# Two feed-forward layers of a float32 encoder trunk, rewritten with Strassen's seven products

## The chip, the cores and the metric

The kernel runs on one core of a Trainium2 chip. The metric is the device time of one execution in microseconds (us). PE is TensorE, DVE is VectorE, ACT is ScalarE, POOL is GpSimd and SP is SyncE, whose queue issues most of the loads.

## The reference

The trunk has two layers on 528 tokens (16 meta tokens, then 512 frames) of width 1024. Layer 0 is multi-scale retention, layer 1 is attention over a shared compressed key and value. Each ends with a dense feed-forward of hidden width 2816:

```python
def swiglu(hn, w1, w3, w2):
    return (jax.nn.silu(hn @ w1) * (hn @ w3)) @ w2

h = h + swiglu(rmsnorm(h, norm_ffn_g[layer]), ffn_w1[layer], ffn_w3[layer], ffn_w2[layer])
```

After layer 1 only the 512 frames are kept, and a last RMSNorm gives the output. All is float32.

## The kernel before

Activations are transposed: features on the 128 partitions (8 tiles for the width, 22 for the hidden width) and tokens along the free axis. A float32 product is three float32r passes over operands that are split into a head and a rest (`split`, L210 to L213: an ACT copy gives the head at L212, a DVE subtraction gives the rest at L208). Weights come as raw tiles of 128x1024 through SP's queue and are split the same way. The ring of weight tiles (`weight_tiles`) has three buffers each for raw, head and rest.

A product (`gemm`) runs over tiles of 128 output columns m. For each m it takes all tiles k of the contraction, and for each k three matmuls (`mm`): for all 528 tokens each is issued in two halves of 264 columns (L246), for 512 frames at once (L248). One matmul has its own weight load in every case.

The feed-forward (`ffn`) has two parts of 11 hidden tiles. Each part computes 22 column tiles of w1 and w3 in turn (`up`), with `evac` after each pair: two DVE products from PSUM with the norm's scale, a Silu on ACT, a DVE product and a split. Then it multiplies with half of w2 (8 column tiles, 11 hidden tiles each) and `add` adds to `h[m]`. In layer 0 the second part's additions are each followed by `prep_mla`, which makes the next stage's operands. In layer 1 the second part is `finish`: the last product, the final norm and the output for half of the frames, then for the other half. In front of the feed-forwards, `prep_ffn` follows the last addition to each `h[m]` in the projections of retention and attention.

The engines' instruction order is made by a scheduler from the program's dependencies and priorities. It isn't the order of the program's text. Semaphores and the reuse of tile buffers come from the same tool.

Before the feed-forwards stand the retention (four heads, some 480 us) and, between the two, the attention (eight heads, some 280 us). In them the change touches memory pools, the shape of some temporary tiles and the order of a few steps.

Of the kernel before, what the change touches and what calls it, by code (L numbers as in the profile page):

```python
# [42 lines left out]
SLOTS = 57  # L43
# [4 lines left out]
# Steps of other work at five places of each head's attention.  # L48
# [9 lines left out]
class Filler:  # L58
    """Steps of independent work, to be put between the steps of a chain."""
# [22 lines left out]
class Head:  # L82
    """One head's attention over tiles of 128 queries, in stages."""
# [37 lines left out]
    def weights(self, i):  # L121
        """The probabilities with keys on partitions, split."""
        k, nc, p = self.k, self.nc, self.p[i]
        qs = slice(i * P, (i + 1) * P)
        if i == 0:
            self.ph = k.tp.tile([P, 4, SEQ], F32R, tag="pth", name=k.name("pth"), bufs=1)
            self.pl = k.tp.tile([P, 4, SEQ], F32R, tag="ptl", name=k.name("ptl"), bufs=1)
            for z in (self.ph, self.pl):
                nc.vector.memset(z.bitcast(F32)[:, 3, 256:384], 0.0)
# [5 lines left out]
        k.split(self.ph[:, : i + 1, qs], self.pl[:, : i + 1, qs], ptv)  # L135
        k.stacked(self.pm[:, qs], pt[:META, 512 : 512 + P], 64)

    def values(self):
# [3 lines left out]
        for j in range(4):  # L142
            vh, vl = (u[:, c] for u in self.v[j])
            q0 = min(j, 2) * P
            ph, pl = self.ph[:, j, q0:], self.pl[:, j, q0:]
            for t, (x, y) in enumerate(((vh, ph), (vh, pl), (vl, ph))):
                nc.tensor.matmul(po[:, q0:SEQ], x, y, start=j == 0 and t == 0, stop=False)  # L147
# [6 lines left out]
class Kernel:  # L154
    """Activations are kept transposed, features on partitions and tokens (16 meta tokens, then
    512 frames) along the free axis. A float32 product is three float32r passes over operands
    split exactly into a 12-bit head and a 12-bit rest."""

    def __init__(self, ctx, tc, a):
# [3 lines left out]
        self.wp = ctx.enter_context(tc.tile_pool(name="wts", bufs=3))  # L163
        self.sp = ctx.enter_context(tc.tile_pool(name="acts", bufs=SLOTS))
        self.tp = ctx.enter_context(tc.tile_pool(name="temps", bufs=4))
        self.small = ctx.enter_context(tc.tile_pool(name="small", bufs=6))
        self.pp = ctx.enter_context(tc.tile_pool(name="psum", bufs=4, space=PSUM))
# [7 lines left out]
    def slot(self, dtype=F32):  # L175
        return self.sp.tile([P, T], dtype, tag="slot", name=self.name("s"))

    def temp(self):
        return self.tp.tile([P, T], F32, tag="tmp", name=self.name("t"))

# [29 lines left out]
    def split(self, hi, lo, src):  # L210
        """src = hi + lo, both float32r."""
# [16 lines left out]
    def weight_tiles(self):  # L228
        return (self.wp.tile([P, WC], F32, tag="raw", name=self.name("raw")),
                self.wp.tile([P, WC], F32R, tag="whi", name=self.name("whi")),  # L230
                self.wp.tile([P, WC], F32R, tag="wlo", name=self.name("wlo")))

    def weights(self, src, n=WC):
        raw, hi, lo = self.weight_tiles()
        self.nc.sync.dma_start(out=raw[:, :n], in_=src)
        self.split(hi[:, :n], lo[:, :n], raw[:, :n])
# [35 lines left out]
    def square_add(self, acc, x, first):  # L272
        """acc += x * x"""
# [8 lines left out]
    def parted(self, acc, full):  # L282
        """acc, split, for half of the work in colsum."""
# [5 lines left out]
    def colsum(self, acc, full):  # L289
        """Sums over partitions, on every partition."""  # L290
# [9 lines left out]
    def rstd(self, r, acc, n, eps, full):  # L300
        """r = 1 / sqrt(sum(acc) / n + eps) on every partition."""
# [13 lines left out]
    def run(self):  # L315
# [7 lines left out]
        self.meta_v = [self.const([80, RDV], F32R, name=f"meta_v{i}") for i in range(2)]  # L323
        self.meta_p = [self.const([80, T], F32R, name=f"meta_p{i}") for i in range(2)]
        for z in self.meta_v + self.meta_p:
            nc.vector.memset(z.bitcast(F32), 0.0)
# [3 lines left out]
        nc.vector.memset(self.eps_gn, GN_EPS)  # L330
        self.retention()
        self.ffn(0, True, self.prep_mla)
        self.mla()
        self.ffn(1, False, None)
# [11 lines left out]
    def prep_ffn(self, layer, k):  # L346
        if k == 0:
            self.acc, self.x = self.slot(), []
        self.x.append(self.prep(k, f"ffn{layer}", self.acc, layer == 0))

    def prep_mla(self, k):
        if k == 0:
            self.acc, self.x, self.xq = self.slot(), [], []
# [650 lines left out]
```

## Time and profile before

| | |
|---|---|
| three runs | 1505.29, 1505.54, 1505.74 us (median 1505.54) |
| profiled execution, span from first to last instruction | 1505.8 us |
| PE, DVE, ACT, POOL busy | 1486.9, 846.7, 571.0, 20.9 us |
| mean granted TensorE clock | 0.997 |

The profiled execution has no other time than its span; it lies 0.3 us above the median of the runs. Busy time of an engine is the union of its instructions. A row of the profile names the line, engine, operation, output and inputs, shape, count, total and mean duration, and what ended the idle time in front. L208 and L212 are the helpers `tt` and `split`, so rows there are told apart by tile names and shapes.

### The profile page before, as it was taken

To read this page: it belongs to the slowest core of one execution; us is meant where nothing else is said; L and a number is where in the kernel's file an instruction comes from. 1 tells how busy PE (TensorE), PEld (TensorE's weight loads), DVE (VectorE), ACT (ScalarE), POOL (GpSimd) and SP (SyncE) were. 2 spreads that over 40 slices of the span, in tenths; PEclk is the share of its full clock that TensorE was granted. 3 is DMA by queue.
4 is the path that set the end of the run, shared out by engine and by line. 5 is a ranking of instruction groups with operands and counts; after the bars stand their busy time and mean duration, and the time that the engine had idled before them with its cause. 6 is when DMAs were issued, how large, how long until landed. Compare 5 with 4: busy or idle time off the path is not lost.

```text
span 1505.8 us, 24568 instructions
## 1 busy us (share of the span) xinstructions
PE 1486.9 (99%) x10450; PEld 1392.0 (92%) x10450; DVE 846.7 (56%) x1286; ACT 571.0 (38%) x946; POOL 20.9 (1%) x44
## 2 busy tenths in 40 slices
PE   8999999999999999999999999999999999999997
PEld 8999999999999999999999998889888888888896
DVE  7665565565577444234445667677885443344464
ACT  5452342342345222123224435666464222222251
POOL 1000000000000000000000000110000000000000
PEclk9999999999999999999999999999999999999998
DMA  5213213213212222332323422321113223323251
GB/s 202 88 47 111 80 46 110 80 48 109 70 58 94 89 88 70 96 112 86 95 67 87 139 84 80 103 67 67 57 44 111 98 81 88 112 98 98 81 160 57
DMA packets 43022, 133.91 MB, mean 89 GB/s; under 512 B 5136, under 2 KB 8720, under 8 KB 42912
## 3 DMA queue, kind: packets, MB, share of 16 engines
q1 hardware_dynamic: 40464, 125.98, 25.7%
q0 software_dynamic: 2448, 6.36, 1.5%
q8 instruction: 82, 1.34, 0.4%
q14 instruction: 28, 0.23, 0.0%
HBM read 128.91 MB, written 2.10 MB: 87 GB/s over the span
## 4 chain that ended last, share of the span: by engine, by line
PE 96%; DVE 1%; ACT 1%; DMA 0%; issue 0%; SPq 0%; DVEq 0%; ACTq 0%
PE ps L246 47%; PE ps L248 28%; PE ps L483 7%; PE ps L915 4%; PE ps L566 2%; PE ps L106 2%; PE ps L524 2%; PE ps L147 1%; PE ps L489 1%; PE ps L491 1%; PE ps L132 1%; PE ps L296 1%; DVE s L208 1%; ACT s L864 0%; DMA s<-w_q 0%; PE ps L567 0%
## 5 line engine op out<-in xcount | busy, mean ns | idle before, releaser
L246 PE MATMUL ps<-s,whi 128*128 128x264 f32 x3904 | 638.2, 285 | 6.5 <-ACT s L224 6.4
L246 PEld LDWEIGHTS ps<-s,whi 128*128 128x128 f32 x3904 | 543.4, 189 | 8.0 <-ACT s L224 6.8
L212 ACT CAST whi<-raw 128x1024 fp32r<-128x1024 f32 (+5 forms) x270 | 246.1, 917 | 652.3 <-PE ps L246 310.2
L246 PE MATMUL ps<-s,wlo 128*128 128x264 f32 x1952 | 398.4, 286 | 0.0
L248 PE MATMUL ps<-s,whi 128*128 128x512 f32 x1248 | 391.9, 395 | 0.5 <-DVE s L208 0.4
L208 DVE TENSOR_TENSOR wlo<-raw,whi 128x1024 fp32r<-128x1024 f32 (+5 forms) x270 | 284.3, 1056 | 107.2 <-ACT whi L212 104.7
L246 PEld LDWEIGHTS ps<-s,wlo 128*128 128x128 f32 x1952 | 303.8, 189 | 0.0
L248 PEld LDWEIGHTS ps<-s,whi 128*128 128x128 f32 x1248 | 232.4, 188 | 54.0 <-DVE s L208 1.0
L248 PE MATMUL ps<-s,wlo 128*128 128x512 f32 x624 | 244.8, 392 | 0.0
L208 DVE TENSOR_TENSOR t<-ps,s 128x528 f32<-128x528 f32 (+1 forms) x120 | 83.0, 700 | 279.8 <-PE ps L246 162.0
L248 PEld LDWEIGHTS ps<-s,wlo 128*128 128x128 f32 x624 | 117.1, 188 | 27.0
L208 DVE TENSOR_TENSOR h<-ps,h 128x528 f32<-128x528 f32 (+2 forms) x100 | 64.9, 653 | 93.3 <-PE ps L246 64.3
L483 PE MATMUL ps<-whi,s 128*128 128x256 f32 x640 | 116.0, 281 | 0.0
L208 DVE TENSOR_TENSOR s<-ps,s 128x256 fp32r<-128x256 f32 (+4 forms) x107 | 59.4, 571 | 89.9 <-ACT s L212 51.5
L483 PEld LDWEIGHTS ps<-whi,s 128*128 128x128 f32 x640 | 99.2, 189 | 0.2
L483 PE MATMUL ps<-wlo,s 128*128 128x256 f32 x320 | 89.7, 280 | 0.0
L483 PEld LDWEIGHTS ps<-wlo,s 128*128 128x128 f32 x320 | 60.4, 189 | 0.0
L212 ACT CAST s<-t 128x528 fp32r<-128x528 f32 (+2 forms) x68 | 40.2, 603 | 48.2 <-DVE t L208 39.4
L208 DVE TENSOR_TENSOR s<-s,s 128x528 fp32r<-128x528 f32 (+4 forms) x85 | 53.7, 657 | 4.9 <-ACT s L212 4.7
L212 ACT CAST s<-ps 128x256 fp32r<-128x256 f32 (+2 forms) x72 | 31.7, 445 | 61.0 <-PE ps L483 50.1
L208 DVE TENSOR_TENSOR s<-t,s 128x528 fp32r<-128x528 f32 (+2 forms) x68 | 44.5, 664 | 8.6 <-ACT s L212 8.4
L212 ACT CAST s<-s 128x528 fp32r<-128x528 f32 (+2 forms) x57 | 32.8, 584 | 39.8 <-DVE s L208 37.3
(140 smaller groups left out, 1105.1 us busy)
## 6 DMA issues: line engine op xcount, KB each, us to landing
raw<-w SPq DMA_DIRECT2D x99, 512.0 KB, 3.5
raw<-w SPq DMA_DIRECT2D x24, 384.0 KB, 3.1
raw<-w_v SPq DMA_DIRECT2D x16, 512.0 KB, 3.8
raw<-w_g SPq DMA_DIRECT2D x16, 512.0 KB, 3.4
raw<-w_ro SPq DMA_DIRECT2D x16, 512.0 KB, 3.4
raw<-w SPq DMA_DIRECT2D x24, 320.0 KB, 2.9
raw<-w_mo SPq DMA_DIRECT2D x8, 512.0 KB, 3.4
raw<-w_q SPq DMA_DIRECT2D x7, 512.0 KB, 4.2
```

The costliest lines, as they stand in the source:

```text
L106: nc.tensor.matmul(out, x[:, qs], y[:, cs], start=t == 0, stop=t == 4 and not masked)
L132: nc.tensor.transpose(pt[:, j * P : (j + 1) * P], p[:, META + j * P : META + (j + 1) * P], k.ident)
L147: nc.tensor.matmul(po[:, q0:SEQ], x, y, start=j == 0 and t == 0, stop=False)
L208: self.nc.vector.tensor_tensor(out=out, in0=a, in1=b, op=op)
L212: self.nc.scalar.copy(out=hi, in_=src)
L246: mm(ps[:, h * 512 : h * 512 + HT], w[p], x[q][:, h * HT : (h + 1) * HT], start=s, stop=e)
L248: mm(ps[:, :SEQ], w[p], x[q], start=s, stop=e)
L296: self.nc.tensor.matmul(ps[:, h * 512 : h * 512 + w], one, z[:, h * w : (h + 1) * w], start=i == 0, stop=i == len(acc) - 1)
L483: mm(ps[:, :256], x[k][p][:, c], w[k][q], start=k == 0 and i == 0, stop=k == last and i == 2)
L524: nc.tensor.matmul(ps[:n, half * 512 : half * 512 + HT], k[d][p][:, t0 : t0 + n], q[d][s][:, half * HT : (half + 1) * HT], start=i == 0, s ...
L566: mm(out, v[j][p][:, c], s[:, c0 : c0 + HT], start=j == 0 and i == 0, stop=False)
L915: nc.tensor.matmul(ps[:, :n], p, q, start=k == 0 and i == 0, stop=k == len(x) - 1 and i == 2)
```

## The change

Both feed-forwards go over to Strassen's scheme in Winograd's form. A unit of work is a `quad`: two tiles of output columns (a tile of w1 and the matching one of w3; or two neighbouring tiles of w2) by two halves of the tokens (264 or 256 columns), with pairs of contraction tiles as the other 2x2 index. Instead of eight block products there are seven (Q1 to Q7), each over `len(xs)` pairs with three passes.

`quad` puts four PSUM banks a, b, d, c to use. Q1 is summed in a, ACT copies it to b, Q6 is added there, ACT copies it to d, Q7 is added to d and Q3 to b. Q5 is made in c and copied to SBUF; one DVE instruction then adds it to b and from d to c. Q4, the last product, is held back: it is issued inside the next quad after that quad's Q5 (`flush`), followed by `done`, the evacuation. The two quads in flight use all eight banks.

`factors` makes the seven weight operands of a quad: four SP loads and two accumulating loads on POOL's queue, two DVE instructions for further sums, then splits of three ring tiles and of one tile of half that size. Two more tiles (`raw2`, one buffer, and a set of `raw4`, two buffers) come from a pool that is open in the feed-forward alone. `operands` makes the seven activation operands of two tiles: four POOL sums, then splits. In `up`, POOL also multiplies by the negated norm scale.

The feed-forward has four parts of 3, 3, 3 and 2 pairs of hidden tiles; before each but the last, one quad of the next part's `up` is issued ahead. `finish` is gone: the final norm follows the last quad for all frames at once. `prep_mla` now follows the whole feed-forward in the text, and layer 1's `prep_ffn` follows the whole attention. Pools are opened and shut by stage; retention has 45 slots and attention 53, where both had 57.

The core of the diff:

```diff
+PARTS = (3, 3, 3, 2)
+    def operands(self, pool, vv, w):
+        add = self.nc.gpsimd.tensor_tensor
+        xp = pool.tile([P, 7, 2, HT], F32R, tag="xp", name=self.name("xp"))
+        tm = self.wide()[:, : 4 * w].rearrange("p (j c) -> p j c", j=4)
+        (b11, b12), (b21, b22) = ((vv[:, i, :w], vv[:, i, w : 2 * w]) for i in range(2))
+        t7, t6, t5, t4 = (tm[:, q - Q7] for q in (Q7, Q6, Q5, Q4))
+        add(out=t5, in0=b11, in1=b12, op=ALU.subtract)
+        add(out=t6, in0=b22, in1=t5, op=ALU.add)
+        add(out=t7, in0=b22, in1=b12, op=ALU.subtract)
+        add(out=t4, in0=t6, in1=b21, op=ALU.subtract)
+        for q, z in ((slice(Q1, Q3), vv[:, :, :w]), (Q3, b22), (slice(Q7, 7), tm)):
+            self.split(xp[:, q, 0, :w], xp[:, q, 1, :w], z)
+        return xp
+    def factors(self, src, n):
...
+        tiles = [self.ring() for _ in range(3)]
+        tiles[1][0] = self.wx.tile([P, WC], F32, tag="raw2", name=self.name("raw2"), bufs=1)
...
+        nc.sync.dma_start(out=r1, in_=src[:, : 2 * n].rearrange("p (j c) -> p j c", j=2))
+        nc.sync.dma_start(out=r3[:, 0], in_=one(1))
+        nc.sync.dma_start(out=r2[:, 1], in_=one(2))
+        nc.sync.dma_start(out=r4, in_=one(3))
+        nc.gpsimd.dma_start(out=r1[:, 1], in_=one(3), accum_op=ALU.add)
+        nc.gpsimd.dma_start(out=r3[:, 0], in_=one(0), accum_op=ALU.add)
+        nc.vector.scalar_tensor_tensor(out=r2[:, 0], in0=r1[:, 0], scalar=-1.0, in1=r1[:, 1],
+                                       op0=ALU.mult, op1=ALU.subtract)
+        self.split(h1, l1, r1)
+        self.tt(r3[:, 1], r2[:, 1], r2[:, 0], ALU.subtract)
+        self.split(h2, l2, r2)
+        self.split(h3, l3, r3)
+        self.split(h4, l4, r4)
...
+    def quad(self, src, xs, w, done):
...
+        product(a, Q1, True, False)
+        nc.scalar.copy(out=b, in_=a)
+        product(c, Q5, True, True)
+        q5 = self.temp()[:, :w]
+        nc.scalar.copy(out=q5, in_=c)
+        self.flush()
+        product(b, Q6, False, False)
+        nc.scalar.copy(out=d, in_=b)
+        product(a, Q2, False, True)
+        product(d, Q7, False, False)
+        product(b, Q3, False, False)
+        self.tt(ps[:, 1::2, :w], ps[:, 1:3, :w], q5[:, None, :].to_broadcast([P, 2, w]), ALU.add)
+        def rest():
+            product(d, Q4, False, False)
+            done(ps[:, 0:2, :w], ps[:, 2:4, :w])
+        self.late = rest
...
+            def done(c1, c2):
+                t = self.temp()[:, :n].rearrange("p (h c) -> p h c", h=2)
+                self.tt(t, c1, rv, ALU.mult)
+                nc.scalar.activation(out=t, in_=t, func=AF.Silu)
+                u = self.temp()[:, :n].rearrange("p (h c) -> p h c", h=2)
+                self.tt(u, c2, t, ALU.mult)
...
+                nc.gpsimd.tensor_tensor(out=vv[:, m % 2].rearrange("p (h c) -> p h c", h=2), in0=u, in1=nv, op=ALU.mult)
+                if m % 2:
+                    hid.append(self.operands(self.hp, vv, w))
...
+    def down(self, part, xs, last):
...
+                    self.tt(h1, c1, h1, ALU.add)
+                    self.tt(h2, h2, c2, ALU.subtract)
+                    if last and not full:
+                        for m in (2 * q, 2 * q + 1):
+                            self.square_add(acc, self.h[m][:, META:], m == 0)
```

## Rows read from the trace of the kernel before

**Rows 1.** Stretches: busy time of each engine with its count, granted clock, DMA:

```profile
core 0: us, PE busy (x) PEld busy (x) DVE busy (x) ACT busy (x) POOL busy (x), PEclk, DMA share, GB/s
478.20:860.30 382.10, 382.10 (x3126) 382.10 (x3126) 169.34 (x204) 115.38 (x148) 1.62 (x3) 1.00 0.29 92
1137.50:1431.50 294.00, 294.00 (x1274) 238.78 (x1273) 128.54 (x153) 83.98 (x106) 0.00 (x0) 1.00 0.29 93
1494.30:1505.80 11.50, 0.70 (x2) 0.30 (x2) 5.85 (x11) 0.89 (x2) 0.00 (x0) 0.64 0.27 91
```

**Rows 2.** Chain that ended last: start, us, what:

```profile
478.19 381.59 PE ps L246 x3120
...
1137.54 294.04 PE ps L248 x1272
1431.57 38.90 PE ps L915 x330
```

**Rows 3.** What PE's matmuls waited for, longest first:

```profile
PE ps L246 <- ACT s L224: 6.4, 1, 6.4
```

**Rows 4.** DVE groups, layer 0's feed-forward: busy us, mean ns:

```profile
L208 DVE TENSOR_TENSOR wlo<-raw,whi 128x1024 fp32r<-128x1024 f32 x43 | 52.6, 1222 | 12.8 <-ACT whi L212 12.4
L208 DVE TENSOR_TENSOR t<-ps,s 128x528 f32<-128x528 f32 x44 | 30.9, 707 | 130.1 <-PE ps L246 130.1
L208 DVE TENSOR_TENSOR wlo<-raw,whi 128x768 fp32r<-128x768 f32 x16 | 15.3, 958 | 0.0
L225 DVE SCALAR_TENSOR_TENSOR s<-h,gains,s 128x512 fp32r<-128x512 f32 x8 | 6.0, 745 | 0.4 <-ACT s L224 0.4
```

**Rows 5.** DVE groups, layer 1's feed-forward:

```profile
L208 DVE TENSOR_TENSOR t<-ps,s 128x512 f32<-128x512 f32 x44 | 30.2, 691 | 117.8 <-PE ps L248 117.7
L208 DVE TENSOR_TENSOR wlo<-raw,whi 128x512 fp32r<-128x512 f32 x12 | 8.0, 686 | 1.7 <-ACT whi L212 1.7
L208 DVE TENSOR_TENSOR h<-ps,h 128x256 f32<-128x256 f32 x16 | 6.7, 420 | 10.7 <-PE ps L915 10.6
L308 DVE RECIPROCAL s<-s 128x512 f32<-128x512 f32 x1 | 3.4, 3354 | 0.8 <-ACT s L306 0.8
L208 DVE TENSOR_TENSOR wlo<-raw,whi 128x384 fp32r<-128x384 f32 x6 | 3.3, 556 | 4.1 <-ACT whi L212 4.0
L886 DVE SCALAR_TENSOR_TENSOR h<-h,gains,s 128x256 f32<-128x256 f32 x8 | 3.2, 476 | 0.0
```

**Rows 6.** DVE in order of time: start us, us:

```profile
708.71 1.22 DVE L208 TENSOR_TENSOR wlo<-raw,whi 128x1024 fp32r<-128x1024 f32 x1
709.84 0.70 DVE L208 TENSOR_TENSOR s<-t,s 128x528 fp32r<-128x528 f32 x1
```

**Rows 7.** ACT groups:

```profile
L212 ACT CAST whi<-raw 128x1024 fp32r<-128x1024 f32 x44 | 46.2, 1050 | 159.4 <-PE ps L246 94.5 <-issue 64.9
L224 ACT ACTIVATE s<-h,gains 128x528 fp32r<-128x528 f32 x8 | 5.9, 739 | 0.6
L306 ACT ACT_TABLE_LOAD x1 | 1.3, 1283 | 0.0
...
L212 ACT CAST s<-ps 128x256 fp32r<-128x256 f32 x16 | 5.8, 371 | 5.9 <-PE ps L483 5.8
```

**Rows 8.** DMA issues: size, median us to landing:

```profile
raw<-w SPq DMA_DIRECT2D x99, 512.0 KB, 3.5
raw<-w SPq DMA_DIRECT2D x24, 384.0 KB, 3.1
...
h<-xT POOLq DMA_DIRECT2D x8, 264.0 KB, 8.3
raw<-w SPq DMA_DIRECT2D x11, 192.0 KB, 2.4
...
s<-qtrig POOLq DMA_DIRECT2D x2, 256.0 KB, 4.5
```

**Rows 9.** What SP's queue waited for:

```profile
SPq L235 <- DVE wlo L208: 1168.6, 223, 17.3
```

More of the change, by code (lines that the diff above doesn't have):

```diff
@@ L172, in name, with pool, shut, slot @@
         return f"{s}_{self.n}"
-    def slot(self, dtype=F32):
-        return self.sp.tile([P, T], dtype, tag="slot", name=self.name("s"))
+    def pool(self, name, side="left", bufs=1, space=None):
+        kw = {"space": space} if space else {}
+        self.n += 1
+        c = self.tc.tile_pool(name=f"{name}{self.n}", bufs=bufs, side=side, reuse_waits="tile", **kw)
+        self.open[name] = c
+        return c.__enter__()
+    def shut(self, *names):
+        for n in names:
+            self.open.pop(n).__exit__(None, None, None)
+    def slot(self, dtype=F32, pool=None):
+        return (pool or self.sp).tile([P, T], dtype, tag="slot", name=self.name("s"))
     def temp(self):
         return self.tp.tile([P, T], F32, tag="tmp", name=self.name("t"))
+    def wide(self, dtype=F32):
+        return self.tp.tile([P, EW], dtype, tag="wide", name=self.name("e"))
+    def bank(self):
+        return self.pp.tile([P, 512], F32, tag="bk", name=self.name("bk"))
     def ps(self):
@@ L226, in split_scaled, with ring @@
             out=lo, in0=src, scalar=scale, in1=hi.bitcast(F32), op0=ALU.mult, op1=ALU.subtract)
[L228 to L231, printed above, removed]
+    def ring(self):
+        return [self.wp.tile([P, WC], dt, tag=t, name=self.name(t))
+                for t, dt in (("raw", F32), ("whi", F32R), ("wlo", F32R))]
     def weights(self, src, n=WC):
-        raw, hi, lo = self.weight_tiles()
-        self.nc.sync.dma_start(out=raw[:, :n], in_=src)
-        self.split(hi[:, :n], lo[:, :n], raw[:, :n])
+        raw, hi, lo = (z[:, :n] for z in self.ring())
+        self.nc.sync.dma_start(out=raw, in_=src)
+        self.split(hi, lo, raw)
         return hi, lo
@@ L346, in prep_ffn @@
     def prep_ffn(self, layer, k):
+        full = layer == 0
+        n = T if full else SEQ
+        v = self.h[k] if full else self.h[k][:, META:]
         if k == 0:
-            self.acc, self.x = self.slot(), []
-        self.x.append(self.prep(k, f"ffn{layer}", self.acc, layer == 0))
+            self.x = []
+        if k % 2 == 0:
+            self.vv = self.wide()[:, : 2 * n].rearrange("p (i c) -> p i c", i=2)
+        self.nc.scalar.activation(out=self.vv[:, k % 2], in_=v, func=AF.Copy, scale=self.g(f"ffn{layer}", k))
+        self.square_add(self.acc[:, :n], v, k == 0)
+        if k % 2:
+            self.x.append(self.operands(self.xp, self.vv, n // 2))
     def prep_mla(self, k):
         if k == 0:
-            self.acc, self.x, self.xq = self.slot(), [], []
+            self.x, self.xq = [], []
         self.x.append(self.prep(k, "kv", self.acc, True))
@@ new lines, in quad, with product @@
+    def quad(self, src, xs, w, done):
+        nc = self.nc
+        fac = self.factors(src, len(xs) * P)
+        ps = self.pp4[self.nq % 2]
+        self.nq += 1
+        a, b, d, c = (ps[:, j, :w] for j in range(4))
+        def product(bank, q, first, last):
+            wt = fac[q]
+            for k, xp in enumerate(xs):
+                cs = slice(k * P, (k + 1) * P)
+                for i, (p, r) in enumerate(((0, 0), (0, 1), (1, 0))):
+                    nc.tensor.matmul(bank, wt[p][:, cs], xp[:, q, r, :w], start=first and k == 0 and i == 0,
+                                     stop=last and k == len(xs) - 1 and i == 2, skip_group_check=True)
+        product(a, Q1, True, False)
[14 more added lines that the diff above has]
+        self.late = rest
@@ L661, in mla @@
     def mla(self):
         nc, a = self.nc, self.a
+        for k in range(KD):
+            self.prep_mla(k)
         acc, xkv, xq = self.parted(self.acc, True), self.x, self.xq
-        r = self.slot()
+        r = self.r
         ktr = self.slot()
@@ L971, in _arrays @@
     for n in range(2):
-        w1, w3 = _blocks(i["ffn_w1"][n]), _blocks(i["ffn_w3"][n])
-        a[f"w13_{n}"] = np.ascontiguousarray(np.stack([w1, w3], 1)).reshape(2 * KH, P, D)
-        a[f"w2_{n}"] = np.stack([_blocks(z) for z in np.split(i["ffn_w2"][n], 2)])
+        w1, w3, w2 = i["ffn_w1"][n], i["ffn_w3"][n], i["ffn_w2"][n]
+        cols = lambda z, m: z[:, m * P : (m + 1) * P]
+        a[f"w13_{n}"] = np.stack([_pair(cols(w1, m), cols(w3, m)) for m in range(KH)])
+        k = 0
+        for part, size in enumerate(PARTS):
+            rows = w2[k : k + 2 * size * P]
+            k += 2 * size * P
+            a[f"w2_{n}_{part}"] = np.stack([_pair(cols(rows, m), cols(rows, m + 1)) for m in range(0, KD, 2)])
     wk = i["mla_w_kv_a"]
```

261 lines of the change are left out of this document (140 added, 121 removed).

## Prediction

> **What bounds the kernel now.** I read the stretches first [rows 1]: in both feed-forwards PE is busy for the whole stretch, at full clock, with one matmul behind another, while DVE is busy for 169.3 of 382.1 us (44%) in layer 0 and 128.5 of 294.0 us in layer 1, and POOL is nearly idle. Then the chain that ended last [rows 2]: it is PE's own queue almost throughout. The list of PE's waits [rows 3] says how little it waits: the longest is 6.4 us, once. So a feed-forward costs its number of matmuls times the price of one:
>
> - 264 columns: 381.59 / 3120 = 122.3 ns [rows 2]. 512 columns: 294.04 / 1272 = 231.2 ns. 256 columns, each with its own weight load as here always: 38.90 / 330 = 117.9 ns.
> - Layer 0: 44 column tiles x 8 x 6 plus 16 x 11 x 6 = 3168 matmuls of 264, 387.4 us. Layer 1: 44 x 24 plus 8 x 33 = 1320 of 512, 305.2 us, and 2 x 8 x 33 = 528 of 256, 62.3 us; 367.5 us.
>
> **What it removes.** A quad has 7 products x pairs x 3 passes: 84 matmuls with four pairs, 63 with three, 42 with two. A layer has 22 quads of four pairs (up), and in down 12 of three and 4 of two: 1848 + 756 + 168 = 2772. Layer 0: 2772 x 122.3 = 339.0, 48.4 saved. Layer 1: 2772 x 117.9 = 326.8, 40.7 saved; the narrower matmuls cost it a little, 0.461 ns per column against 0.452. Together **-89.1 us**, if PE stays as gapless as now. The few extra matmuls (norm sums, four that prepare banks) are under 2 us.
>
> **What it adds to DVE.** A row's duration overstates what an instruction takes in a full queue: the 1.22 us split at 708.71 was followed at 709.84 [rows 6], so I take 0.09 off each row: 1.13 for a split of 1024, 0.87 for 768, 0.60 for 512, 0.47 for 384, 0.33 for 256, 0.62 for an evacuation of 528, 0.66 for a scaled sum of 512 [rows 4, 5]. An up quad in layer 0 then needs for weights 3 x 1.13 + 0.60 + 0.66 + 0.60 = 5.25, for three instructions at PSUM 1.86, and for half of the operands of a pair (528, 264 and 1056 columns) 1.06: 8.17 us, against PE's 84 x 0.1223 = 10.27. Down quads: 5.94 against 7.70 (three pairs) and 4.71 against 5.14 (two). Layer 0: 22 x 8.17 + 12 x 5.94 + 4 x 4.71 = 270 of 339 us. Layer 1 by the same sum: 8.08 against 9.90, 5.88 against 7.43, 4.65 against 4.95; 272 of 327 us. In its last four quads the squares add two sums of 0.60: 5.85 against 4.95. So DVE goes from 44% to some 80%: no longer free, not yet the bound. ACT has 3 x 1.05 + 0.62 for weights, three copies of about 0.37, a Silu (some 0.65) and half of a pair's heads (1.07) [rows 7]: 6.6 of 10.27.
>
> **Buffers and waits inside a quad.** All three head and rest buffers belong to one quad, so there is no spare set. But each is free early: the first after Q5, the second after Q2, the third after Q3, and each is wanted again five products later: 5 x 1.47 = 7.3 us for a split that takes 2.2. The copy from b to d must fit under Q2: 0.37 plus an ACT instruction in the way (1.05) against 1.47; with two pairs Q2 is 0.73 us and may lose some tenths, eight times. DVE's sum over b and d has Q1 and Q5 of the next quad, 2.9 us, for 0.7.
>
> **What it adds to POOL.** No row shows POOL on data. Below I take DVE's row for the same shape (0.71 for 528 columns, 0.42 for 264), above the slowest row of that length (the reciprocal, 3.35 for 512, so 3.45, and half of that for 264) [rows 4, 5]. I take twice the lower end, 1.4 and 0.85: nearer to the row of the same operation. Two up quads then have 2 x 1.4 + 4 x 0.85 = 6.2 us of POOL in 20.5; even the upper end fits (13.8).
>
> **The loads.** Each quad's sum needs a load, then an accumulating load, then a split. Plain loads of these sizes land in 3.5 us (512 KB), 3.1 (384 KB) and, between 320 and 192 KB rows, 2.7 (256 KB); for an accumulating one I take POOL's 4.5 (256 KB), with 2.4 (192 KB, SP) below and 8.3 (264 KB, eight at a time) above [rows 8]. SP's loads already wait for buffers, 223 times [rows 9], with no harm to PE. A raw tile is held 3.5 + 4.5 + 1.05 + 1.13 + 0.66 = 10.8 us, and one that is loaded second about 10. The ring hands out three raw tiles to a quad of which two get data. If the third can serve the next quad, 20.8 us of use on 3 x 10.27 is no limit; with two pairs 17.5 / 3 = 5.8 against 5.05, a loss of 0.8 x 8 = 6 us. Half of this and the tenths above I take as hidden by work issued ahead: **+5** for waits in the steady state (0 to 40).
>
> **What it moves.** Before, the operands of the next stage were made between products; now they stand behind them, and here PE has nothing else to do:
>
> - Into layer 0's feed-forward: after the last addition (0.7) a scale (0.74), four POOL sums (3.4), heads and rests of 1056 columns (2.3): 7.1 us until Q5 can run, of which Q1 covers 1.5 and earlier operands some. **+5** (0 to 9).
> - Into the attention: eight times two scaled sums and a square's sum on DVE, 0.67 + 0.62 + 0.66 = 1.95, in all 15.6 us, and four last quads with 0.4 us to spare each. The new product takes tiles one by one. **+8** (0 to 16).
> - Into layer 1's feed-forward: as in layer 0, but the operands' memory was the attention's, and the last product reads part of that to its end. **+7** (0 to 14).
> - The end: before, PE's last matmul was followed by 11.5 us [rows 1], with half of the frames to go through. Now all 512: two additions and two squares (2.7), sums over partitions (0.7, the PE time of rows 1's last stretch), a table load (1.28) and two roots (some 0.45 each) [rows 7], reciprocal 3.35 [rows 5], eight products of 0.66 (5.3), and the last output, about 4 as now: 18.3, so +7; and the last quads lose 4 x 0.9 to DVE. **+10** (6 to 16).
> - Retention and attention: fewer slots, 16 more small splits on ACT and DVE: **+2** (-4 to 10).
>
> Sum: -89.1 + 5 + 5 + 8 + 7 + 10 + 2 = **-52**. The profiled span, 1505.8, is 0.3 over the runs' median; 1505.5 - 52 gives **1454 us**.
>
> **A rule that speaks against it.** The DVE splits read two operands from SBUF, and POOL's sums read SBUF too; the trace has no instant with both, so it says nothing on their getting in each other's way. The Trainium skill (SBUF — State Buffer, Who interferes with whom) states that a DVE instruction with two SBUF inputs and a GpSimd instruction that reads SBUF lock each other out of a shared port for the whole instruction. No run here shows that yet; by it the time is that of the first rival. The Trainium skill (GPSIMD Engine Reference, Elementwise — side-by-side cycle accounting) gives the two engines' addition at 4497 and 2293 ns for 2048 columns; by that ratio of 1.96 my POOL prices, twice DVE's, would stand as they are.
>
> **The rivals.**
>
> 1. *DVE becomes the bound, held up by POOL.* POOL's work is 22 x 1.4 + 44 x 0.85 = 68 us a layer, 3.1 per up quad. 77% of DVE's time per quad goes to instructions with two SBUF inputs; if these wait for POOL, DVE needs 8.17 + 2.4 = 10.57 against 10.27 (and 10.48 against 9.90): 22 x 0.3 + 22 x 0.58 = 19, for the 5 of my waits: 1468; with a full queue's own jitter some 1475. At POOL's upper price (6.9 per up quad, 5.3 of it on DVE) it is 44 x 3.4 = 150 and 1600; it turns into a loss at 4.2 us of POOL per up quad. For: 80% before any such wait. Against: POOL has idle time to wait in, and DVE's PSUM work to slip behind.
> 2. *The accumulating loads bound the quads (slower).* If the unused raw tile holds a buffer, a raw buffer serves one quad at a time: 6.3 + 4.5 = 10.8 against 10.27 and 9.90 (31 us), 5.3 + 4.5 = 9.8 against 7.57 (24 x 2.2 = 53), 4.3 + 4.5 = 8.8 against 5.05 (30): 114 in place of 5, **1563**. It decides against the change from 3.7 us per accumulating load on. For: the price is unseen, and POOL's queue holds these loads behind its sums. Against: three buffers for two loads.
> 3. *The seams cost nothing:* the scheduler finds cover for all but the end: -89 + 8 = 1425.
>
> **Chances.** Forecast (1436 to 1472) 0.50; rival 1 0.20, a quarter of it slower; rival 2 0.11; rival 3 0.14; the rest, mixtures near no change, 0.05. Faster by over 0.2% (3 us, about what a measurement tells here): 0.82; within it 0.03; slower 0.15. Range 1422 to 1500: below it a twentieth, above it the slower cases.
>
> **What would show it.** Right: some 2772 matmuls a layer at 122 and 118 ns in unbroken stretches of about 10.3 and 9.9 us per quad; DVE at 80%; PE gaps of several us at three seams and an end of 18 us. Rival 1: PE waiting for rests on DVE in every up quad, and DVE's splits above 1.22 us beside POOL. Rival 2: PE or DVE waiting for loads, accumulations above 4 us, worst in down. Wrong altogether: a matmul whose price changes when it adds into a copied bank, or a clock that falls in the gaps, as the 0.64 of the last stretch [rows 1].

## Result and profile after

The change makes the kernel slower: median 1760.0 us (1749.7 to 1760.2) against 1505.5, ratio 1.167, 95% interval 1.164 to 1.170. The prediction was 1454 (1422 to 1500). One execution of five took 7938 us, with its matmuls several times as far apart for a reason that no run shows, and it was the one profiled with these runs, so the rows of after come from a second profile of the same kernel (the run after_again, span 1761.9 us).

The page's first lines: span, busy time and share of each engine, instruction counts, and the granted clock in 40 slices.

```profile
span 1761.9 us, 27975 instructions
PE 1527.9 (87%) x10988; PEld 1434.3 (81%) x10988; DVE 1171.1 (66%) x1661; ACT 775.5 (44%) x1365; POOL 323.1 (18%) x360
...
PEclk9999999999899999999988999999899989999987
```

PE is no longer busy throughout. The two feed-forwards from their first to their last product, three microseconds of one of them, and the end (the columns of [rows 1]):

```profile
472.00:956.10 484.10, 397.76 (x2777) 371.39 (x2776) 321.28 (x392) 209.07 (x341) 137.15 (x146) 0.93 0.53 126
632.50:635.60 3.10, 3.10 (x15) 3.10 (x15) 1.49 (x2) 0.00 (x0) 0.00 (x0) 0.50 0.39 112
1252.70:1743.10 490.40, 388.68 (x2778) 363.61 (x2776) 320.36 (x391) 209.37 (x346) 140.90 (x147) 0.92 0.50 119
1743.10:1761.90 18.80, 2.58 (x6) 1.00 (x4) 11.41 (x13) 3.49 (x5) 0.00 (x0) 0.55 0.30 112
```

The counts are right: 2772 matmuls a layer and a few more. But they take 484.1 and 490.4 us, where the prediction had 339.0 and 326.8 for PE alone: 308.7 us more. Against [rows 1 and 2] these two stretches grew by 484.1 - 382.1 + 490.4 - 356.8 = 235.6 us; the attention between them, 296.6 us, by 19.4, and the end by 7.3; the first feed-forward began 6.2 us earlier. Together 256.1, the difference of the spans.

Neither DVE (66%) nor any other engine is full, so PE waits for order, not for capacity. What PE's matmuls waited for (total us, times, longest), in place of the one wait of [rows 3]:

```profile
PE b L734 <- DVE b L233: 61.1, 44, 3.4
PE b L734 <- ACT b L738: 55.3, 23, 3.8
...
PE b L734 <- ACT b L744: 31.6, 69, 1.1
```

L738 is the ACT copy from a to b, L744 the copy from b to d, and "DVE b" the sum over b and d that must come before Q4. All three are short instructions of the quad itself, not heads or rests of weights. The starts of the copies at L738 lie 11.5 to 15.6 us apart in most up quads (forecast 10.3 and 9.9) and 10 to 13 us in down quads of three pairs (7.7 and 7.4).

I added up the starts of the 5544 quad matmuls. 264 of them came 0.245 us or more after the one before, 240 us beyond the usual 0.122; the matmul behind each such wait came 0.23 after it, another 28 us; and 464 ran in trains 0.22 us apart, 46 us. That is 314 us, the whole loss within the counting. The trains stand behind the longer waits, nearly all of them behind one of 2 us or more: in the second row of the windows above, behind a wait of 2 us, the granted clock is 0.50, the lower of the two levels, 1.2 GHz.

### The profile page after: what moved, and what is told of

Same layout as the page of the kernel before. It is cut to its first block, busy times and chain, and to the rows that moved or that the text cites. A ratio compares the mean times of both kernels' runs of the same rounds, so it can differ in the third digit from the quotient of the medians.

```text
span 7936.7 us, 27975 instructions
## 1 busy us (share of the span) xinstructions
PE 7862.8 (99%) x10988; PEld 7440.8 (94%) x10988; DVE 1135.0 (14%) x1661; ACT 786.1 (10%) x1365; POOL 302.5 (4%) x360
## 4 chain that ended last, share of the span: by engine, by line
PE 99%; ACT 0%; DVE 0%; POOL 0%; issue 0%; DMA 0%; ACTq 0%; DVEq 0%; POOLq 0%
PE b L734 47%; PE ps L271 23%; PE ps L273 9%; PE ps L539 8%; PE ps L622 2%; PE ps L113 2%; PE ps L580 2%; PE ps L156 1%; PE ps L139 1%; PE ps L545 1%; PE ps L547 1%; PE ps L321 1%; PE ps L623 0%; PE ps L140 0%; ACT b L744 0%
## 5 line engine op out<-in xcount | busy, mean ns | idle before, releaser
L734 PE MATMUL b<-xp,whi 128*128 128x264 f32 (+1 forms) x3696 | 3180.4, 1050 | 46.2 <-ACT b L744 23.2
L734 PEld LDWEIGHTS b<-xp,whi 128*128 128x128 f32 x3696 | 2930.9, 929 | 105.5 <-ACT b L744 56.8
L734 PE MATMUL b<-xp,wlo 128*128 128x264 f32 (+1 forms) x1848 | 1906.9, 1038 | 0.0
L734 PEld LDWEIGHTS b<-xp,wlo 128*128 128x128 f32 x1848 | 1731.7, 942 | 0.8 <-issue 0.8
L271 PE MATMUL ps<-s,whi 128*128 128x264 f32 x1824 | 1418.1, 1056 | 7.4 <-ACT whi L237 6.6
L271 PEld LDWEIGHTS ps<-s,whi 128*128 128x128 f32 x1824 | 1352.6, 920 | 14.7 <-ACT whi L237 6.6
L271 PE MATMUL ps<-s,wlo 128*128 128x264 f32 x912 | 791.5, 1055 | 0.0
L271 PEld LDWEIGHTS ps<-s,wlo 128*128 128x128 f32 x912 | 730.2, 920 | 0.8 <-issue 0.8
L539 PE MATMUL ps<-whi,s 128*128 128x256 f32 x640 | 550.3, 1035 | 0.0
L539 PEld LDWEIGHTS ps<-whi,s 128*128 128x128 f32 x640 | 517.8, 943 | 2.7 <-issue 2.6
L273 PEld LDWEIGHTS ps<-s,whi 128*128 128x128 f32 x368 | 328.0, 914 | 135.1 <-issue 133.0
L273 PEld LDWEIGHTS ps<-s,wlo 128*128 128x128 f32 x184 | 166.3, 904 | 75.5 <-issue 73.5
L707 POOL DMA_DIRECT2D raw<-w x76 | 66.2, 871 | 3911.5 <-DMA raw<-w 3883.9
```

Of the source, the lines that this page charges most:

```text
L271: mm(ps[:, h * 512 : h * 512 + HT], w[p], x[q][:, h * HT : (h + 1) * HT], start=s, stop=e)
L273: mm(ps[:, :SEQ], w[p], x[q], start=s, stop=e)
L539: mm(ps[:, :256], x[k][p][:, c], w[k][q], start=k == 0 and i == 0, stop=k == last and i == 2)
L734: nc.tensor.matmul(bank, wt[p][:, cs], xp[:, q, r, :w], start=first and k == 0 and i == 0, stop=last and k == len(xs) - 1 and i == 2, skip ...
```

## The experiments

All ratios are against the kernel before, run beside each on the same chip.

**The unchanged kernel, the loads, POOL.** First the parts that the rivals name.

after_again: nothing edited.

> The changed kernel unchanged, for a trace at its usual speed. Every theory: 1750 to 1760 us, and a matmul of 264 columns again at some 122 ns where PE does not wait. The trace should say what PE waits for: loads theory, a raw tile or its accumulating load; POOL theory, the operands and rests that stand behind POOL's sums on DVE; order theory, short waits inside every quad for an ACT copy or a DVE sum whose engine is held by something else.

1761.7 us, 1.170 (1.167 to 1.173).

```diff
-        nc.gpsimd.dma_start(out=r1[:, 1], in_=one(3), accum_op=ALU.add)
-        nc.gpsimd.dma_start(out=r3[:, 0], in_=one(0), accum_op=ALU.add)
```

> The two accumulating loads of each quad are left out, so the weight sums lack those terms; everything else stays. Loads theory: most of the 250 us over the kernel before goes, and the 50 forecast come in: 1455 to 1530 us. POOL theory and order theory: within 40 us of 1758.

1706.9 us, 1.134 (1.130 to 1.137): 55 us.

```diff
-        add(out=t5, in0=b11, in1=b12, op=ALU.subtract)
...
-        add(out=t4, in0=t6, in1=b21, op=ALU.subtract)
+        tm = vv.rearrange("p i (h c) -> p (i h) c", h=2)
...
-                nc.gpsimd.tensor_tensor(out=vv[:, m % 2]..., in0=u, in1=nv, op=ALU.mult)
+                self.tt(vv[:, m % 2]..., c2, t, ALU.mult)
```

> POOL's sums are left out: the four operand sums (the splits read the same number of columns of the two tiles themselves) and the product with the negated norm scale (DVE writes its product there directly). POOL theory: 1455 to 1530 us. Loads theory and order theory: within 40 us of 1758.

1662.0 us, 1.104 (1.101 to 1.107): 100 us below after_again, as the 55 are (98 below the first runs' 1760.0). Each is a part; neither is the loss. Both together, in the next run:

> Leaves out the two accumulating loads of each quad and also the POOL operand sums and POOL's product with -r (operand splits read the hidden tile instead), so the output is not the reference's. If the two costs measured one at a time (55 and 98 us) are separate and all that there is besides is something else: 1762 - 55 - 98 = 1609. If each hides behind the other (either keeps the quads late, so taking one away shows too little), and nothing else holds PE up: near the forecast, 1450 to 1480. Order theory (PE's short waits for the ACT copies of PSUM banks and the DVE sum, held up by what stands in front of them on ACT and DVE): between 1560 and 1610, with PE's waits for those copies still in the list.

1603.3 us, 1.065 (1.062 to 1.068). The two simply add up (1762 - 55 - 100 = 1607), and 149 us above the forecast remain that neither has to do with: up quads take 11.8 us in layer 0, and those from 533 to 556 us have three short waits each, for the ACT copies at this run's L731, L734 and L737.

**Weights or copies.** Two runs that take away everything of one kind.

```diff
-        fac = self.factors(src, len(xs) * P)
+        if self.fac is None:
+            self.fac = self.factors(src, 4 * P)
+        fac = self.fac
```

> Loads, sums and splits the weights of one quad per layer and uses them for all quads of the layer (all other weights of the feed-forward left out, so the output is not the reference's). PSUM copies, the DVE sum, evacuations and POOL's operand sums stay. If the feeding of weights (loads, accumulating loads, splits and their place in DVE's and ACT's order) is the cause: 1440 to 1490. If the PSUM copies are late for reasons of their own (POOL's sums before the operand casts on ACT): 1600 to 1700.

1620.2 us, 1.076 (1.071 to 1.081).

```diff
-        nc.scalar.copy(out=b, in_=a)
...
-        nc.scalar.copy(out=q5, in_=c)
...
-        product(b, Q6, False, False)
-        nc.scalar.copy(out=d, in_=b)
+        product(b, Q6, True, False)
...
-        product(d, Q7, False, False)
+        product(d, Q7, True, False)
...
-        self.tt(ps[:, 1::2, :w], ps[:, 1:3, :w], q5[:, None, :].to_broadcast([P, 2, w]), ALU.add)
```

> Leaves out the two ACT copies from bank to bank, the ACT copy of Q5 and the DVE sum over two banks (the products Q6 and Q7 start their banks anew), so the output is not the reference's; the seven products, all loads, splits, POOL's work and the evacuations stay. Theory that PE's waits inside a quad for these are the loss: 1440 to 1520. Theory that the weights come late (accumulating load, raw tile and split in DVE's order, a loop of some 13.6 us in the trace): 1680 to 1760, with PE then waiting for heads and rests of the weights instead.

1671.6 us, 1.110 (1.104 to 1.117). Neither theory holds alone: with no weights to feed the time is still 166 us above the forecast, with PE waiting for the sum over b and d (36.1 us) and the copy from b to d (24.7); with no copies PE waits for rests of the weights instead (48.8 us).

**The raw tiles' loop.** The timeline of after between two issues of the same load (L703 is a quad's first load, L707 the accumulating load on top of it, L709 DVE's scaled sum of weights):

```profile
619.75 0.33 SPq L703 DMA_DIRECT2D raw<-w  x1
...
624.99 0.86 POOL L707 DMA_DIRECT2D raw<-w  x1 [4.86 <-DVE wlo L233]
...
629.89 0.28 PE L734 MATMUL b<-xp,wlo 128*128 128x264 f32 x1
...
630.86 0.69 DVE L709 SCALAR_TENSOR_TENSOR raw<-raw 128x512 f32<-128x512 f32 x1 [2.60 <-DMA raw<-w]
631.47 0.71 DVE L233 TENSOR_TENSOR b<-b,t 128x528 f32<-128x528 f32 x1
632.09 1.22 DVE L233 TENSOR_TENSOR wlo<-raw,whi 128x1024 fp32r<-128x1024 f32 x1
632.23 0.75 PE L734 MATMUL b<-xp,whi 128*128 128x264 f32 x2 [2.06 <-DVE b L233]
...
633.33 0.33 SPq L703 DMA_DIRECT2D raw<-w  x1
```

From the plain load's issue to the accumulating one's are 5.2 us, from there to L709 5.9; DVE stands idle for it 2.60 us, and behind L709 in DVE's order stand the sum over b and d, for which PE waits 2.06 us, and the split at whose end the next L703 is issued, since it frees the tile. The loop is 633.33 - 619.75 = 13.6 us, against 10.3 of matmuls. A fourth raw tile should open it:

```diff
-        return [self.wp.tile([P, WC], dt, tag=t, name=self.name(t))
+        return [self.wp.tile([P, WC], dt, tag=t, name=self.name(t), bufs=RING + (t == "raw"))
```

> Four raw weight tiles in the ring in place of three, nothing else. If the raw tile that a quad's third load hands to the load two quads later (free only when DVE has passed the next quad's scaled sum, which waits for its accumulating load) closes the loop of 13.6 us: it should give back at least what leaving out the accumulating loads did, 1680 to 1710. If the tiles are not what the loop hangs on: 1750 to 1765.

1709.0 us, 1.135 (1.132 to 1.138): 53 us, as much as leaving the accumulating loads out. L709's wait for its load, 52.3 us in after, is gone from the list of waits. But DVE's wait for the load of the second raw tile grew from 14.5 to 65.4 us: with this loop open, the next one holds.

**Waits on other banks.** The compiled order of PE tells what no wait list does. One up quad of the changed kernel, the matmuls that carry a wait, of Q1, Q5, the late Q4, Q6, Q2 and Q7 in turn (this is the list of instructions, not the profile; the number in front is not a count of matmuls, of which each product has 12):

```
4169 L734 MATMUL b_0_5380<-xp_5125,whi_8384 128x264 [waits DVE_49]
4178 L734 MATMUL b_0_5380<-xp_5125,whi_8384 128x264 [waits Activation_49]
4187 L734 MATMUL b_0_5379<-xp_5125,whi_1075_8258 128x264 [waits DVE_49]
4196 L734 MATMUL b_0_5380<-xp_5125,whi_8387 128x264 [waits Activation_49]
4205 L734 MATMUL b_0_5380<-xp_5125,whi_8387 128x264 [waits Activation_49]
4215 L734 MATMUL b_0_5380<-xp_5125,wlo_8391 128x264 [waits DVE_49]
```

Q5 writes bank c but waits for the copy from a to b; Q2 writes a but waits for the copy from b to d. The four banks are one tile, and the products wait as if its banks were one. Q6 waits for the copy of Q5 to SBUF as well, which reads bank c. So each copy stands bare between two products. With a tile for each bank, Q5 and Q2 lose that wait, and Q6 and Q7, which need the copies, keep it:

```diff
-        self.pp4 = [pool.tile([P, 4, 512], F32, tag=f"b{i}", name=f"b{i}_{layer}") for i in range(2)]
+        self.pp4 = [[pool.tile([P, 512], F32, tag=f"b{i}{j}", name=f"b{i}{j}_{layer}") for j in range(4)]
+                    for i in range(2)]
...
-        self.tt(ps[:, 1::2, :w], ps[:, 1:3, :w], q5[:, None, :].to_broadcast([P, 2, w]), ALU.add)
+        self.tt(b, b, q5, ALU.add)
+        self.tt(c, d, q5, ALU.add)
```

> Each quad's four PSUM banks are four tiles of one bank in place of one tile of four banks; the sum over b and d, the evacuations and the additions to h are then two instructions of 264 columns each in place of one of 528 (about 0.42 us more DVE per quad). In the compiled order of PE before this edit, the first matmul of Q5, of Q6 and of Q2 wait for ACT, that is each product waits for the copy made just before it, though it touches other banks; with the edit only Q6 and Q7 wait, one product later. If these waits are what is left when POOL's sums and the accumulating loads are away (some 1.6 us a quad there, 76 quads): about 120 us less than 1760, 1640 to 1670. If the copies are late because of what stands before them on ACT, and the waits would come a product later all the same: 1740 to 1770.

1689.9 us, 1.122 (1.119 to 1.126): 72 us, less than expected while the loop is still closed. With the fourth raw tile:

> One-bank PSUM tiles and four raw weight tiles together; correct result, nothing left out. If the raw tiles' loop (51 us by itself) and the waits for copies on other banks (120 us) are separate: 1760 - 51 - 120 = 1590. If each hides behind the other: more is gained, 1520 to 1560. If the copies are late for what stands before them on ACT: 1700.

1596.8 us, 1.061 (1.057 to 1.064): 112 us below raw4. And with the loads and POOL's work away:

> One-bank PSUM tiles, without the accumulating loads and without POOL's sums and its product with -r (the output is not the reference's). If three things together, the loop through the raw tiles, POOL's sums and the waits for copies on other banks, make up the whole loss: 1603 - 120 = 1483 or less, near the forecast of 1454 with 5 to 30 us for the seams. If there is a fourth: above 1540.

1476.1 us, 0.980 (0.978 to 0.983). Its stretches between the first and the last copy from a to b:

```profile
472.40:808.70 336.30, 333.46 (x2713) 332.54 (x2713) 285.58 (x483) 197.16 (x322) 1.62 (x3) 0.99 0.43 128
1122.70:1451.20 328.50, 326.67 (x2722) 324.92 (x2722) 283.18 (x481) 197.01 (x325) 0.00 (x0) 0.99 0.42 126
```

PE is busy for 99% again, up quads take 10.3 and 9.9 us, down quads 7.7 and 7.5. So three things make up the loss; there is no fourth of any size. Its feed-forwards take 22 us more than their matmuls, most of it at their starts and around their last parts.

**How POOL costs time.** First by the order of ACT: the splits of hidden tiles are issued behind the copy from b to d, a quad later.

```diff
+            self.pend.append(splits)
...
+        if pend:
+            with self.tc.issue_after(cp.ins):
+                pend()
```

> As the one-bank tiles with four raw tiles, and besides the splits of each pair of hidden tiles are issued one quad later, behind the copy from b to d, so that ACT does not stand waiting for POOL's sums in front of a PSUM copy (not for the last pair of a part). Result unchanged. If POOL's lateness works through ACT's order: 40 to 60 us less than without. If through DVE's slower splits beside POOL: within 10 us of it.

1575.0 us, 1.046 (1.043 to 1.049): 22 us, half of what that theory asked for, and the edit moves DVE's splits as well as ACT's. Then POOL works on, but between a feed-forward's own quads nothing reads its results:

```diff
-                nc.gpsimd.tensor_tensor(out=vv[:, m % 2]..., in0=u, in1=nv, op=ALU.mult)
+                    self.tt(vv[:, m % 2, h * w : (h + 1) * w], c2[h], t[:, h], ALU.mult)
+                nc.gpsimd.tensor_tensor(out=self.tm[:, :n]..., in0=vv[:, m % 2]..., in1=nv, op=ALU.mult)
```

> One-bank PSUM tiles with four raw tiles, where POOL computes the same products and sums as before at the same shapes, but nothing reads the results in the feed-forward: DVE writes the hidden tile without -r, and the operand splits read it directly (the output is not the reference's). If POOL costs time because ACT's and DVE's splits, and with them the PSUM copies behind them, stand waiting for its results: 1490 to 1520 against 1597, as without POOL's work. If it costs time by slowing DVE's instructions that run beside it: 1570 to 1600. In between, the two shares can be read off.

1590.5 us, 1.056 (1.053 to 1.059): only 6 us less than with the results read. That does not clear the late results: with them read (bank_raw4) ACT waits 112 us for POOL, and DVE's splits of hidden tiles, 1056 and 528 columns, take 1258 and 890 ns; unread, ACT waits 10 us, but the same splits, now beside POOL's sums, take 1722 and 1652. The run exchanges one cost for the other, and how POOL's 77 us (1596.8 - 1519.7, a run below) divide between the two where its results are read stays open. In bank_raw4:

```profile
ACT xp L237 <- POOL e L806: 57.9, 22, 3.3
ACT xp L237 <- POOL e L687: 54.3, 27, 2.8
```

```profile
L233 DVE TENSOR_TENSOR xp<-e,xp 128x1056 fp32r<-128x1056 f32 x15 | 18.9, 1258 | 16.9 <-ACT xp L237 16.9
...
L233 DVE TENSOR_TENSOR xp<-e,xp 128x528 fp32r<-128x528 f32 x15 | 13.3, 890 | 20.6 <-ACT xp L237 20.6
```

What POOL's work costs where nothing waits for it can be measured. The timeline of pool_unread, in order (L705 is the load of the second raw tile):

```profile
615.21 1.43 DVE L233 TENSOR_TENSOR wlo<-raw,whi 128x1024 fp32r<-128x1024 f32 x1
...
616.66 0.33 SPq L705 DMA_DIRECT2D raw<-w  x1
...
620.69 0.69 DVE L233 TENSOR_TENSOR raw<-raw 128x512 f32<-128x512 f32 x1 [1.98 <-DMA raw<-w]
621.30 0.77 DVE L233 TENSOR_TENSOR t<-b,r 128x264 f32<-128x264 f32 x2
...
622.10 0.64 ACT L800 ACTIVATE t<-t 128x528 f32<-128x528 f32 x1 [4.48 <-DVE t L233]
622.65 0.37 ACT L744 COPY b<-b 128x264 f32<-128x264 f32 x1
...
623.07 0.59 PE L734 MATMUL b<-xp,whi 128*128 128x264 f32 x1 [3.06 <-ACT b L744]
```

A split, 0.2 us longer than alone, ends at 616.64 and frees the one buffer of the second raw tile; its load is issued, lands 3.9 us later, and DVE's sum of weights can run; behind that stands the evacuation, behind that the Silu, behind that the copy from b to d, and PE has waited 3.06 us. I first took the load in this chain for an accumulating one, late because it stood behind POOL's sums in that engine's queue; it is a plain load of SP's. Two runs make four corners with the two before: POOL's work unread or absent, accumulating loads there or not.

> The kernel with POOL's work unread and one-bank tiles and four raw tiles, now also without the two accumulating loads of each quad (the output is not the reference's). POOL then does the same products and sums, at the same shapes, beside DVE, and nothing at all waits for POOL. If POOL's sums cost time because the accumulating loads stand behind them in POOL's queue (a chain seen in the trace: sum, load, DVE's sum of weights, DVE's evacuation, ACT's Silu, ACT's copy, PE): 1475 to 1485, as without POOL's work at all (1476). If they cost time by slowing DVE's instructions: 1540 to 1580, and little less than the 1590 with the loads.

1530.9 us, 1.017 (1.015 to 1.019).

> One-bank tiles, four raw tiles, accumulating loads kept, POOL's sums and its product with -r left out as in the first runs (the output is not the reference's), so that POOL only issues loads. It is the fourth corner to three runs: POOL's work unread with the loads 1590 and without 1531, neither 1476. If the 60 us of the loads come from standing behind POOL's sums in its queue: 1476 to 1485. If the loads cost the same by themselves, through the raw tiles that they hold: 1530 to 1540, as 1476 + 60. If they cost only together with DVE's slowed splits, which free the second raw tile late: 1480 to 1500.

1519.7 us, 1.009 (1.006 to 1.012).

| | with accumulating loads | without |
|---|---|---|
| POOL's work, unread | 1590.5 | 1530.9 |
| no POOL work | 1519.7 | 1476.1 |

The last corner has three raw tiles, the others four; four were not tried there. 1530.9 and 1519.7 lie between the ranges expected, so neither theory holds pure. The loads cost 44 us by themselves and 60 beside POOL's sums: POOL's queue is at most 16 of it, and my theory of that queue falls. POOL's work costs 55 us without the loads, and 71 with them. Not all of it is work that nobody waits for: the operands that enter a feed-forward still come from POOL's sums, and in unread_no_accum ACT waits for those 12.8 us, six times, each time before the first copy from a to b. Between that copy and the last one of the layer, where nothing waits for POOL, it costs 40 us of the 55, and there DVE is busy for 633.0 us in place of 568.8. In all four corners DVE's wait for the second raw tile goes with the loads: 103.0 and 123.9 us with them, 37.4 and 27.8 without.

DVE's groups in unread_no_accum (busy us, mean ns), POOL at work:

```profile
L233 DVE TENSOR_TENSOR wlo<-raw,whi 128x1024 fp32r<-128x1024 f32 x220 | 285.9, 1301 | 36.2 <-ACT whi L237 34.0
L233 DVE TENSOR_TENSOR xp<-e,xp 128x1056 fp32r<-128x1056 f32 x15 | 24.9, 1660 | 3.4 <-ACT xp L237 3.4
L233 DVE TENSOR_TENSOR xp<-e,xp 128x528 fp32r<-128x528 f32 x15 | 23.2, 1550 | 1.9 <-ACT xp L237 1.9
```

and of bank_no_both, POOL idle:

```profile
L233 DVE TENSOR_TENSOR wlo<-raw,whi 128x1024 fp32r<-128x1024 f32 x220 | 268.4, 1221 | 49.8 <-ACT whi L237 46.9
...
L233 DVE TENSOR_TENSOR xp<-e,xp 128x1056 fp32r<-128x1056 f32 x15 | 18.8, 1257 | 2.4 <-ACT xp L237 2.1
...
L233 DVE TENSOR_TENSOR xp<-e,xp 128x528 fp32r<-128x528 f32 x15 | 10.5, 702 | 2.0 <-ACT xp L237 2.0
```

The same splits of 528 columns take 1550 in place of 702 ns where POOL's sums run beside them.

**Taking the work off POOL.** Two tiles of two banks (a with b, d with c) instead of four, with the late Q4 between Q6 and Q2 so that each copy has a product on the other tile behind it, and evacuations in one instruction again:

```diff
-        self.flush()
         product(b, Q6, False, False)
         nc.scalar.copy(out=d, in_=b)
+        self.flush()
```

> Two PSUM tiles of two banks (a with b, d with c) for each quad and the last product of the quad before set between Q6 and Q2 in place of between Q5 and Q6, so that each copy has a product on the other tile behind it; four raw tiles; evacuations at 528 columns again (0.4 us less DVE per quad than with one-bank tiles). POOL as in the change. Theory that POOL is what is left: 1580 to 1600, as with one-bank tiles. If DVE's time per quad mattered: 1550 to 1570.

1610.9 us, 1.069 (1.065 to 1.074): 14 us above the one-bank tiles, a miss; PE waits 53.6 us for the copy from a to b, longest 5.6. Why this order suffers more from POOL I did not settle. With the sums on DVE:

```diff
-        add = self.nc.gpsimd.tensor_tensor
+        add = self.nc.vector.tensor_tensor
```

> As the two-bank tiles with four raw tiles, and the four operand sums of each pair on DVE in place of POOL (POOL keeps the product with -r and the accumulating loads). DVE by the rows: 8.2 + 0.1 + 0.85 = 9.2 us of 10.3 per up quad. If POOL's sums are what keeps the quads late: 1500 to 1530. If DVE is then the bound: 1540 or more, with PE waiting for rests.

1575.1 us, 1.046 (1.043 to 1.049): the range for DVE as the bound. The next step speaks against that, since it gives DVE still more to do. With the product too (`nc.gpsimd` to `nc.vector` at L802):

> As before, and the product with -r on DVE too, so that POOL only issues loads. DVE by the rows: 9.9 us per up quad against PE's 10.3 and 9.9. If POOL's lateness or its effect on DVE is worth more than 0.7 us of DVE per quad: below the run with the sums alone on DVE, 1480 to 1510. If DVE is the bound: above it, 1520 to 1550.

1523.9 us, 1.012 (1.005 to 1.018): the last 51 us come from one product of 1.4 us per up quad on POOL, for 0.7 us more on DVE. What DVE still waits for in this run:

```profile
DVE raw L233 <- DMA raw<-w: 62.9, 42, 3.8
```

That sum of weights reads the second raw tile, which has one buffer. Its loaded half in two buffers:

```diff
-        tiles[1][0] = self.wx.tile([P, WC], F32, tag="raw2", name=self.name("raw2"), bufs=1)
+        r2 = [self.wx.tile([P, WC // 2], F32, tag=t, name=self.name(t), bufs=k)[:, :n] for t, k in (("raw2a", 1), ("raw2b", 2))]
```

> The version with two-bank tiles, four raw tiles and POOL's sums and its product on DVE (1524), in which the second raw weight tile is two tiles of 512 columns, the loaded one of them in two buffers, so that this load need not wait for the split of the quad before (SP's third load of a quad waits for DVE for 207 us in all in that version, and DVE's sum of weights then for the load). DVE has one more split of 512 for one of 1024, 0.1 us more. If that load holds up the quads: 1490 to 1510. If DVE's 10 us per quad are the bound: 1520 to 1530.

**1489.8 us** (1488.8 to 1490.6), 0.990 (0.988 to 0.991): faster than the kernel before. Its two feed-forwards from the first to the last product:

```profile
468.30:823.10 354.80, 346.10 (x2778) 343.01 (x2776) 321.61 (x535) 213.77 (x377) 63.74 (x75) 0.98 0.70 173
1120.10:1467.60 347.50, 339.19 (x2777) 334.22 (x2777) 320.01 (x541) 214.01 (x383) 62.08 (x72) 0.98 0.68 165
```

DVE is busy for 321.6 of 354.8 us (in after 321.3 of 484.1), and PE gains by the change: up quads take 10.2 and 9.9 us. That wait for the second raw tile is gone.

## Why the prediction was wrong

- **PE's saving of 89.1 us: right.** The counts are as worked out, and where nothing holds PE up, quads take 10.2 to 10.3 us and 9.9 (forecast 10.27 and 9.90).
- **Unit prices: nearly right.** POOL's product of 528 columns took 1413 ns (taken: 1.4 us), its sums of 264 columns 1034 to 1140 (taken: 0.85); an accumulating load of 256 KB 4.9 us (taken: 4.5). DVE's 8.17 us per up quad gave 270 us for layer 0; with POOL idle (bank_no_both) it was 285.6 in the stretch, in a version that makes two instructions of each sum over b and d and each evacuation.

```profile
L802 POOL TENSOR_TENSOR e<-t,acc 128x528 f32<-128x528 f32 x22 | 31.1, 1413 | 12.1 <-DVE t L233 11.9
...
L687 POOL TENSOR_TENSOR e<-e,e 128x264 f32<-128x264 f32 x15 | 15.5, 1034 | 0.0
```

```profile
raw<-w POOLq DMA_DIRECT2D x88, 256.0 KB, 4.9
```

- **"+5 for waits in the steady state (0 to 40)": the step that failed.** The feed-forwards took 308.7 us more than their matmuls; the fast version's take 36.5 more (354.8 + 347.5 - 665.8), most of it at seams. The step compared each engine's sum with PE's and took what fits as hidden. In a fixed order an engine that stands waiting holds up all that is queued behind it. Taken off one after another, from 1762: a fourth raw tile 53, a tile for each bank 112, POOL's results unread 6, no POOL work 71, no accumulating loads 44: 1476. The shares go with this order; the bank tiles alone, taken first, gave 72.
- **"The copy from b to d must fit under Q2": wrong.** Q2 itself waits for it, and Q5 for the copy from a to b. I had read the dependence off the banks; the program tracks the tile. This is the largest share, and no rival had it.
- **Raw tiles.** The prediction had a tile held 10.8 us and three tiles for two loads. The loop was 13.6 us: the accumulating load took 5.9 there, and the split that frees the tile stood behind the next quad's L709 in DVE's order. The second raw tile, which has one buffer, was not in the sum at all: load, wait and split make a loop of their own, and a second buffer gave 34 us. Rival 2 named the loads (114 us); a fourth raw tile gave 53 us, and leaving the accumulating loads out at the end another 44.
- **Rival 1, DVE held up by POOL: right in kind.** It asked for 19 us of waits, or 26 with jitter; measured, POOL's work is 55 (71 with the accumulating loads), 40 of the 55 between the first and the last copy of the two layers (354.1 + 351.1 against 336.3 + 328.5), the rest around them, where the first operands still wait for POOL's sums. DVE's rows with two inputs from SBUF grew (702 to 1550 ns); its evacuations from PSUM stayed at 703 in after. The Trainium skill (SBUF — State Buffer, Who interferes with whom) states just this, that a DVE instruction with two SBUF inputs and a GpSimd instruction that reads SBUF lock each other out; these rows agree. I saw the rule and weighed it at 0.20, because POOL has idle time to wait in; but DVE's long row is the one that others queue behind. In after itself ACT also waits 81.9 us for POOL's results; how much of the loss is this and how much the slower DVE rows stays open.
- **Clock.** The prediction named a clock that falls in the gaps as a way to be wrong. Trains at 0.22 us per matmul added some 46 us in after, 5 in the fast version.
- **Seams.** The end was 18.8 us (forecast 18.3). The attention's stretch grew by 19.4, by 19.8 in the fast version (1120.1 - 823.1 against 277.2). But before, 48 matmuls of layer 1's feed-forward ran in that stretch (1320 by the prediction's count, 1272 from 1137.54 on [rows 2]), 11.1 us at 231.2 ns, and the saving of 89.1 counts them. Without them the stretch grew by 30.5 and 30.9, where the prediction had 8 and 2. (The same holds for 48 matmuls of layer 0 before 478.2: they are 5.9 of the 6.2 us by which its feed-forward began earlier.) One seam was not in the sum at all: into the last down part, whose operands come from the last up quad. From the last up quad's copy on, the fast version shows:

```profile
782.80:823.10 40.30, 35.27 (x256) 33.64 (x254) 35.09 (x72) 23.42 (x50) 5.96 (x8) 0.92 0.50 141
1430.80:1467.60 36.80, 33.63 (x255) 31.88 (x254) 32.44 (x66) 20.90 (x47) 4.30 (x5) 0.95 0.27 62
```

At 122.3 and 117.9 ns these matmuls are 31.3 and 30.1 us, so 16 us went there. With the attention's 21 beyond the forecast this is as much as separates 1490 from 1454; smaller differences go both ways.

## What to carry to other kernels

A sum of busy times per engine is a bound only if nothing in any queue waits; before giving "0" to waits, write down one period of each queue in order and follow each cross-engine chain round to where it starts again: here load, accumulating load, scaled sum, split, free tile, load. Ask of each dependence what the program tracks, the bank or the tile, since a copy with a product meant to cover it can stand bare. An engine at 90% without waits beat one at 66% that shared its work with POOL.

## Unexpected in the hardware

- A wait costs more than itself: the matmul behind it came 0.23 us after the first one in place of 0.122, and after the 2 us wait shown above the granted clock was 0.50 over 3.1 us.
- POOL suffers from DVE as DVE does from POOL: L687's sum of 264 columns took 1034 ns on average in after and 1596 in pool_unread, where it runs beside DVE's splits of hidden tiles, one of 1056 columns taking 1.81 us in place of 1.26.
- Moving one POOL instruction of 1.4 us per up quad to DVE, at 0.7 us there, took 51 us off the kernel, 1.2 us for each of the 44, although DVE's work grew by 0.7 us each time.
